# Logsumexp over heads: two more constant products on TensorE, the checks of three batches and one logarithm moved into or behind the hand list, and the last rows planned anew

## The chip, the cores and the metric

The kernel runs on one core of a Trainium2 chip. The metric is the device time of one execution in microseconds (us). Input and output lie in the chip's HBM; a core has TensorE (PE in the profile, its weight loads PEld), VectorE (DVE), ScalarE (ACT), GpSimd (POOL) and SyncE (SP, which here only issues transfers). Each engine works through its own instructions in order.

## The reference

`x` is 8 x 2048 x 2048 in f32 (134 MB), `bias` 8 x 256. A row of 2048 numbers is 8 heads of 256:

```python
B, S, D = x.shape
H = bias.shape[0]
Dh = D // H
x_heads = x.reshape(B, S, H, Dh).transpose(0, 2, 1, 3)
x_heads = x_heads + bias[None, :, None, :]
x_tiled = np.repeat(x_heads, 2, axis=2)
mx = x_tiled.max(axis=-1, keepdims=True)
lse = mx.squeeze(-1) + np.log(np.exp(x_tiled - mx).sum(axis=-1))
```

For each row and head: the logarithm of the sum of exp(x + bias) over 256 numbers, written twice. The output is 8 x 8 x 4096 in f32, 1 MB.

## The kernel before

**Units and loads.** The 16,384 rows are cut into 64 units of 256 rows (two rows on each of 128 partitions, 2 MB), eight units for a batch. They pass through four tiles `xb` of two units each. Units 2 to 41 (`BLOCKS` = 42) come as 4 MB loads of two units, so the last 4 MB block is units 40 and 41; units 42 to 56 come as 2 MB, 57 to 60 row by row as 1 MB, and 61 to 63 (`T_TAIL` = 61) in the parts of `TAIL_LOADS` (unit, row of the pair, first head, last head). All loads are issued on SP's queue, each once the unit that had its buffer is done.

**One unit of the bulk (units 0 to 53).** Nothing is subtracted ahead of the exponential. The eight heads go three ways:

- Heads 0 to 2: TensorE puts the bias into PSUM (`put_bias`, L356, a product of a matrix of ones with the bias, L370, issued a unit ahead) and adds x by a product with the identity (`late_heads`, L423, products L428). ACT takes the exponential from PSUM, head 0 with its sum (L439), heads 1 and 2 back into `xb` (L446).
- Heads 4 to 7: POOL adds the bias in place (`g_add`, L478).
- Head 3: no bias is added; ACT's exponential takes heads 3 to 7 in one instruction (L484), and DVE then multiplies head 3 by exp(bias), which lies in PSUM as `w_ps` (L496).

DVE sums heads 1 to 7 in one reduction (L503). So the order for a unit is: load; TensorE and POOL; ACT; DVE; its buffer is free.

**Later units.** 54 to 56 add fewer heads on TensorE; 57 to 60 go row by row: heads 0 and 1 as TensorE and ACT sums (L405, L459), the others as exponential (L484) and then multiplied by exp(bias) and summed by DVE (`weigh`, L519), with one head folded on POOL: multiplied (L536) and halved three times (L542), the last 32 numbers summed by DVE (`add_folded`, L549). In these units `keep_warm` (L418) issues a product of the identity with 384 constant columns of the bias into `tp`, which nothing reads.

**The hand list.** The six rows of units 61 to 63 are called e, f (61), a, b (62), c, d (63), and `TAIL` gives the order in which their steps are issued. A word such as `add a:12` means heads 1 and 2 of row a. `add`: TensorE adds x to a bias that was put into a PSUM bank ahead of it (`next_bias`, L799; the addition L821). `sum`: ACT's exponential from PSUM with its sum (L459). `copy`: ACT's exponential from PSUM into `xb` (L832). `exp`: ACT's exponential in place (L484). `weigh`: DVE's multiplication with exp(bias) and sum. `whole`: DVE's sum of 256 numbers (L845; no word of the old list uses it). `fold .0` to `.3`: POOL's multiplication and halvings, `folded`: DVE's sum of what is left. `sums`, `rest`: work left from unit 60. `warm`: `keep_warm`.

**Logarithms and stores.** The sums of batches 0 to 3 and 4 to 5 (the "groups") are turned by TensorE into `tp` and put through ACT's logarithm by `finish` (L564, the logarithm L578), two units after the group's last one; for batches 4 and 5 that is at unit 49. Batch 6 has its transposes in `turn_two` (L708) behind unit 57 and its logarithm in `finish_two` (L720) behind unit 58, in a bank of the PSUM tiles `pair`. Batch 7 is `finish_last` (L728), after the list: a transpose of the 128 x 128 sums, the logarithm, and a store on ACT's queue. `on_bank` enters the users of a bank, so that users of the other bank of the same tile don't wait for each other; the transpose in `finish_last` is not entered. `store` (L580) issues the stores of the groups and of `res_two` (batch 6) on SP's queue ahead of the list.

**Checks.** Without a maximum subtracted, a sum could overflow or vanish. So the exponent bits of all sums are looked at: `ends_of` (L592) reduces a group's bits to their largest and smallest on DVE and puts these two words beside the sums of the next group; `see_before` (`seen6`) looks at batch 6 with its two extra words, `see_early` (`seen7`) at the units of batch 7 that are done by then, `judge` (L642) at the rest; `gather` (L622) counts the odd bits by products with ones, and if there are any, `all_again` (L662) computes the whole output anew in the safe way. The verdict is loaded by SP and the others at the end.

Of the kernel before, what the change touches and what calls it, by code (L numbers as in the profile page):

```python
# [9 lines left out]
F32 = mybir.dt.float32  # L10
# [9 lines left out]
BLOCKS = 42  # L20
# [36 lines left out]
    (62, 1, 2, 8),  # L57
    (63, 1, 1, 6),
    (62, 0, 0, 5),
    (63, 1, 6, 8),  # L60
    (62, 0, 5, 8),
    (63, 0, 5, 8),
    (63, 1, 0, 1),
    (63, 0, 2, 5),
    (63, 0, 0, 2),
    (62, 1, 0, 1),
    (62, 1, 1, 2),
# [5 lines left out]
sums  add e:0  warm  exp e:1234567  # L73
rest  seen6  sums  fold e:67.0  weigh e:1  sum e:0
weigh e:2  add f:01  exp f:34567  weigh e:3  weigh e:4
fold e:67.1  weigh e:5  add f:2  sum f:0  seen7  weigh f:7  sum f:1
fold e:67.2  exp b:34567  weigh f:3  fold e:67.3  add b:2  weigh f:4
weigh f:5  weigh f:6  sum f:2  fold b:67.0  weigh b:3
add d:1  warm  exp d:2345  weigh b:4  weigh b:5
folded e:67  sum b:2  weigh d:2  fold b:67.1  sum d:1  weigh d:3  add a:12  # L80
exp a:34  weigh d:4  fold b:67.2  weigh d:5  exp d:67
weigh a:3  fold b:67.3  add a:0  seen  copy a:12  weigh a:4  weigh d:7
exp a:567  fold a:12.1  weigh d:6
folded b:67  sum a:0  weigh a:7  fold a:12.2  exp c:567  add d:0  weigh a:5
fold a:12.3  weigh a:6  sum d:0  weigh c:5  fold c:7.0  add c:2
exp c:34  weigh c:6  folded a:12  add c:0  exp c:1  fold c:7.1  weigh c:3
sum c:2  weigh c:4  fold c:7.2  add b:0  exp b:1  weigh c:1  fold c:7.3  sum c:0
weigh b:1  sum b:0  folded c:7
# [4 lines left out]
def kernel(  # L93
# [44 lines left out]
    odd = sb.tile([P, 2 + NR + H * SEEN], I32, name="odd")  # L138
# [8 lines left out]
    pads = [1] * (len(widths) - 1) + [0]  # L147
# [19 lines left out]
    sb.tile([P, 48], F32, name="gap")  # L167
# [412 lines left out]
    def store():  # L580

        for (b0, b1), r in zip(groups, res):
            nc.sync.dma_start(
                out=out[b0:b1].rearrange("b h (n r) -> (b h n) r", n=NB),
                in_=r.rearrange("q p k r -> q (p k r)"),
            )
        nc.sync.dma_start(
            out=out[B - 2].rearrange("h (n r) -> (h n) r", n=NBLK),
            in_=res_two.rearrange("q p k r -> q (p k r)"),
        )  # L590
# [44 lines left out]
    def see_before():  # L635
        odd_bits(odd[:, 0 : 2 + NR], Rx[len(groups)].bitcast(I32))

    def see_early():
        to = odd[:, 2 + NR :].rearrange("p (h c) -> p h c", h=H)
        odd_bits(to, last_bits(0, SEEN))  # L640
# [79 lines left out]
    def finish_two():  # L720
        (bank,) = two_in
        two = ps[bank][0 : H * NBLK]
        tv = bass.AP(
            tensor=two.tensor, offset=two.offset, ap=[two.ap[0], [1, P], [P, K], [0, 2]]
        )
        on_bank(bank, nc.scalar.activation(out=res_two, in_=tv, func=ACT.Ln))

# [131 lines left out]
    for t in range(T_TAIL):  # L859
# [4 lines left out]
        for k0, k1, c0, c1 in pieces(t):  # L864
# [4 lines left out]
            if m["late"]:  # L869
                pe_part = late_heads(m, t, bias_here, sums)  # L870
            else:
# [50 lines left out]
            if m["g0"] < H:  # L922
# [3 lines left out]
                if m["late"]:  # L926
                    bias_there = put_bias(*next_units.pop(0))
            else:
                for_pe.extend(pe_parts)

        for i, (_, b1) in enumerate(groups):
            if t - 2 == b1 * NBLK - 1:
                finish(i)
                ends_of(i)
        if t == T - 7:
            turn_two()
        if t == T - 6:
            finish_two()
# [9 lines left out]
    for what, row, heads, step in tail:  # L948
        if row is None:
# [3 lines left out]
                "seen6": see_before,  # L953
                "seen7": see_early,
                "seen": lambda: gather(odd, True, False),
# [5 lines left out]
    assert not for_pe and not for_pool and not to_bias  # L961
    finish_last()
# [35 lines left out]
```

## Time and profile before

| | |
|---|---|
| median of 3 runs | 322.71 us (322.35 to 322.72) |
| the profiled execution | 322.78 us |
| its span, first to last instruction | 321.0 us |
| its mean granted TensorE clock | 0.945 of full speed |
| busy: PE, DVE, ACT, POOL | 77%, 89%, 82%, 90% |
| read from HBM, written | 134.23 MB, 1.05 MB; 421 GB/s over the span |

Times are in us from the first instruction of the profiled execution. A row of the timeline is: start, length, engine, line, operation, output<-inputs, count, and in brackets the idle time before it with what ended it. A row of the chain of waits is: start, length, what. A row of busy time by stretch is: stretch, its length, the busy time of each engine with its instructions, the granted TensorE clock (1.00 is full speed), the share of time in which the DMA engines were busy, and GB/s. A row of a group of instructions is: what, count, then its busy time and the mean ns of one, then the idle time before them. The last loads wait in SP's queue for their buffers long before they move, so their time from issue to landing says little by itself; where a load lands is seen by the instruction that waits for it.

### The profile page before, as it was taken

How to read it: one execution, taken by the hardware profiler on the slowest of the kernel's cores; microseconds unless marked ns; L12 is line 12 of the kernel's file. 1: busy time of each engine (PE TensorE's matmuls, PEld its weight loads, DVE VectorE, ACT ScalarE, POOL GpSimd, SP SyncE). 2: the span in 40 equal slices, each digit the busy share in tenths (PEclk: the TensorE clock that was granted, in tenths of full speed). 3: DMA queues.
4: the chain of work that ended last, by engine and by line, in shares of the span. 5: the costliest groups of instructions: out<-in, count | busy, mean ns of one | idle time of the engine just before them, and what ended most of it. 6: DMA issues, size and time to landing. Idle time of an engine off the chain costs nothing.

```text
span 321.0 us, 2284 instructions
## 1 busy us (share of the span) xinstructions
PE 247.9 (77%) x618; PEld 100.3 (31%) x618; DVE 286.6 (89%) x304; ACT 264.0 (82%) x437; POOL 287.5 (90%) x116
## 2 busy tenths in 40 slices
PE   5998784867868687866979776698877788398773
PEld 2333331323323233322323332233332233143232
DVE  2347999699998989999799999979999999999996
ACT  1159986888879878888698988869988898999995
POOL 7939997999999999999999989999999999977874
PEclk9979998999979989997797999969999999979999
DMA  7999999999999999999999999999999999999995
GB/s 309 464 404 457 416 434 451 396 457 445 404 453 433 422 447 400 453 445 405 453 434 421 449 419 433 423 427 431 435 435 430 423 431 432 422 429 428 422 413 193
DMA packets 8950, 135.44 MB, mean 422 GB/s; under 512 B 996, under 2 KB 1511, under 8 KB 2791
## 3 DMA queue, kind: packets, MB, share of 16 engines
q1 hardware_dynamic: 8784, 135.14, 98.4%
q10 hardware_dynamic: 152, 0.14, 0.1%
q8 instruction: 5, 0.08, 0.1%
q14 instruction: 9, 0.07, 0.1%
HBM read 134.23 MB, written 1.05 MB: 421 GB/s over the span
## 4 chain that ended last, share of the span: by engine, by line
DVE 44%; DMA 34%; PE 11%; ACT 6%; POOL 3%; issue 1%; SPq 0%
DMA xb<-in_x_dram 34%; DVE R L503 30%; DVE xb L519 9%; DVE xb L496 4%; PE pair L428 4%; ACT xb L484 4%; PE one_ps L428 3%; POOL xb L478 3%; PE pair L303 1%; ACT xb L446 1%; PE pair L370 1%; PE one_ps L370 1%; DVE R L598 1%; DMA brow<-in_bias_dram 1%; DVE R L549 0%
## 5 line engine op out<-in xcount | busy, mean ns | idle before, releaser
L478 POOL TENSOR_TENSOR xb<-xb,b_rep 128x2048 f32<-128x2048 f32 x57 | 257.6, 4543 | 19.5 <-DMA xb<-in_x_dram 19.4
L503 DVE TENSOR_REDUCE R<-xb 128x14 f32<-128x3584 f32 (+1 forms) x57 | 216.8, 3804 | 1.9
L484 ACT ACTIVATE xb<-xb 128x2560 f32<-128x2560 f32 (+8 forms) x79 | 156.9, 1998 | 17.0 <-POOL xb L478 16.9
L428 PE MATMUL pair<-xb,ident 128*128 128x512 f32 x216 | 111.5, 642 | 0.0
L428 PE MATMUL one_ps<-xb,ident 128*128 128x512 f32 x108 | 63.0, 668 | 17.6 <-DMA xb<-in_x_dram 17.5
L446 ACT ACTIVATE xb<-pair 128x1024 f32<-128x1024 f32 x54 | 55.5, 1028 | 19.2 <-PE pair L428 19.1
L428 PEld LDWEIGHTS pair<-xb,ident 128*128 128x128 f32 x216 | 45.4, 210 | 59.2 <-issue 59.2
L496 DVE TENSOR_TENSOR xb<-xb,w_ps 128x512 f32<-128x512 f32 x54 | 36.7, 680 | 23.2 <-ACT xb L484 23.2
L370 PE MATMUL one_ps<-b,ones_bf 128*128 128x512 bf16 x52 | 20.1, 387 | 36.2 <-ACT xb L439 36.1
L439 ACT ACTIVATE xb<-one_ps 128x256 f32<-128x256 f32 x108 | 40.0, 379 | 7.0 <-PE one_ps L428 7.0
L370 PEld LDWEIGHTS <-ones_bf 128*128 128x128 bf16 (+1 forms) x174 | 17.5, 101 | 84.5 <-issue 77.6
L370 PE MATMUL pair<-b,ones_bf 128*128 128x512 bf16 x104 | 31.2, 381 | 0.0
L428 PEld LDWEIGHTS one_ps<-xb,ident 128*128 128x128 f32 x108 | 19.5, 198 | 32.7 <-DMA xb<-in_x_dram 26.5
L439 ACT ACTIVATION_READ_ACCUMULATOR xb<-one_ps 128x1 f32 x108 | 22.1, 205 | 0.0
L519 DVE CUSTOM_DVE_ANT_0 xb<-xb,w_ps 128x256 f32<-128x256 f32 x60 | 22.0, 414 | 0.0
L405 PE MATMUL pair<-xb,ident 128*128 128x512 f32 x28 | 16.0, 672 | 6.0 <-DMA xb<-in_x_dram 5.9
L542 POOL TENSOR_TENSOR xb<-xb 128x128 f32<-128x128 f32 (+3 forms) x36 | 14.2, 394 | 3.3 <-ACT xb L832 0.5
L459 ACT ACTIVATE xb<-pair 128x256 f32<-128x256 f32 x39 | 15.2, 417 | 0.0
L536 POOL TENSOR_TENSOR xb<-xb,w_sb 128x256 f32<-128x256 f32 (+1 forms) x11 | 9.1, 828 | 4.6 <-ACT xb L484 4.1
L821 PE MATMUL pair<-xb,ident 128*128 128x256 f32 (+1 forms) x22 | 8.0, 456 | 3.3 <-DMA xb<-in_x_dram 3.1
L459 ACT ACTIVATION_READ_ACCUMULATOR xb<-pair 128x1 f32 x39 | 9.6, 245 | 0.0
L405 PEld LDWEIGHTS pair<-xb,ident 128*128 128x128 f32 x28 | 4.9, 197 | 12.4 <-DMA xb<-in_x_dram 10.3
(61 smaller groups left out, 84.8 us busy)
## 6 DMA issues: line engine op xcount, KB each, us to landing
xb<-in_x_dram SPq DMA_DIRECT2D x20, 4096.0 KB, 22.3
xb<-in_x_dram SPq DMA_DIRECT2D x17, 2048.0 KB, 21.6
xb<-in_x_dram SPq DMA_DIRECT2D x10, 1024.0 KB, 21.1
xb<-in_x_dram SPq DMA_DIRECT2D x2, 640.0 KB, 18.1
xb<-in_x_dram SPq DMA_DIRECT2D x3, 384.0 KB, 12.3
xb<-in_x_dram SPq DMA_DIRECT2D x1, 768.0 KB
xb<-in_x_dram SPq DMA_DIRECT2D x2, 256.0 KB, 15.4
out_dram<-res SPq DMA_DIRECT2D x1, 512.0 KB, 5.8
```

The lines of the kernel that those rows point to most:

```text
L370: nc.tensor.matmul(p, lhsT=lhsT, rhs=each_row(b, h * Dh, Dh, K), start=i == 0, stop=False,)
L405: mm = nc.tensor.matmul(p, lhsT=ident, rhs=xts[t % NBUF][:, ka:kb, c : c + w], start=False, stop=True,)
L428: mm = nc.tensor.matmul(p, lhsT=ident, rhs=xts[t % NBUF][:, :, h * Dh : (h + 1) * Dh], start=False, stop=True,)
L439: act = nc.scalar.activation(out=xts[t % NBUF][:, k, 0:Dh], in_=got[0][:, k * Dh : (k + 1) * Dh], func=ACT.Exp, accum_out=sums[:, k, 0:1],)
L446: act = nc.scalar.activation(out=xts[t % NBUF][:, :, Dh : m["pe"] * Dh].rearrange("p k (h j) -> p h k j", j=Dh), in_=got[-1].rearrange("p ...
L459: act = nc.scalar.activation(out=xts[t % NBUF][:, k, h * Dh : (h + 1) * Dh], in_=p, func=ACT.Exp, accum_out=sums[:, k, h : h + 1],)
L478: add = nc.gpsimd.tensor_tensor(out=v, in0=v, in1=each_row(b_rep, c - G0, D - c, k1 - k0), op=ALU.add)
L484: return on_x(t, nc.scalar.activation(out=v, in_=v, func=ACT.Exp), [after])
L496: mul = nc.vector.tensor_tensor(out=f, in0=f, in1=each_row(w_ps, m["pe"] * Dh - W0, n, k1 - k0), op=ALU.mult,)
L503: red = nc.vector.tensor_reduce(out=sums[:, k0:k1, h0:H], in_=v.rearrange("p k (h j) -> p k h j", j=Dh), op=ALU.add, axis=mybir.AxisListTy ...
L519: ttr = nc.vector.tensor_tensor_reduce(out=v, in0=v, in1=w, scale=1.0, scalar=0.0, op0=ALU.mult, op1=ALU.add, accum_out=dst,)
L542: done = nc.gpsimd.tensor_tensor(out=v[:, :, 0:n], in0=v[:, :, 0:n], in1=v[:, :, n : 2 * n], op=ALU.add)
```

## The change

Four things are done.

1. At unit 39, the last one ahead of the last 4 MB block, `keep_warm` is issued twice: once behind that unit's identity products (`late_heads`) and once behind the bias products for unit 40 (`put_bias`).
2. The checks of batches 4 and 5 no longer go through two end words. `ends_of` is called for the first group alone (after unit 33), so its pair of reductions behind unit 49 goes. In the list, `seen5` (`see_groups`) turns the 258 words of batches 4 and 5 (their sums and the two end words of batches 0 to 3) in place into their odd bits; by then their logarithm is long taken. `seen6` (`see_two`) takes the 128 words of batch 6; `seen` (`gather_seen`) gathers both. `odd` and the sums of batch 6 are two words shorter each, and the unused tile `gap` grows from 48 to 64 words, so that `xb` lies at the address that it had.
3. `turn_two` and `finish_two` are called after the list, just ahead of `finish_last`, and the store of batch 6 with them: it is no longer issued by `store` ahead of the list.
4. `TAIL_LOADS` and `TAIL` are new. In numbers of instructions: 30 `weigh` become 29 and 2 `whole`, with 4 `folded` in both; 11 `sum`, 11 `exp` and 1 `copy` become 9, 12 and 3; 15 steps of `fold` become 14; 11 `add` (13 heads) become 12 (15 heads); the 2 `warm` go. The parts of `TAIL_LOADS` remain 13, with the same 6 MB; the first two (rows e and f) stay.

```diff
--- before.py
+++ after.py
@@ -54,38 +54,39 @@
 TAIL_LOADS = [
     (61, 0, 0, 8),
     (61, 1, 0, 8),
-    (62, 1, 2, 8),
-    (63, 1, 1, 6),
-    (62, 0, 0, 5),
-    (63, 1, 6, 8),
-    (62, 0, 5, 8),
-    (63, 0, 5, 8),
-    (63, 1, 0, 1),
-    (63, 0, 2, 5),
+    (63, 1, 2, 8),
+    (62, 0, 2, 8),
+    (62, 1, 2, 6),
+    (63, 0, 4, 8),
+    (63, 1, 0, 2),
+    (62, 1, 6, 8),
+    (62, 1, 1, 2),
+    (62, 0, 0, 2),
+    (63, 0, 2, 4),
+    (62, 1, 0, 1),
     (63, 0, 0, 2),
-    (62, 1, 0, 1),
-    (62, 1, 1, 2),
 ]
 
 ROWS = {"e": (61, 0), "f": (61, 1), "a": (62, 0), "b": (62, 1), "c": (63, 0), "d": (63, 1)}
 
 TAIL = """
-sums  add e:0  warm  exp e:1234567
-rest  seen6  sums  fold e:67.0  weigh e:1  sum e:0
-weigh e:2  add f:01  exp f:34567  weigh e:3  weigh e:4
-fold e:67.1  weigh e:5  add f:2  sum f:0  seen7  weigh f:7  sum f:1
-fold e:67.2  exp b:34567  weigh f:3  fold e:67.3  add b:2  weigh f:4
-weigh f:5  weigh f:6  sum f:2  fold b:67.0  weigh b:3
-add d:1  warm  exp d:2345  weigh b:4  weigh b:5
-folded e:67  sum b:2  weigh d:2  fold b:67.1  sum d:1  weigh d:3  add a:12
-exp a:34  weigh d:4  fold b:67.2  weigh d:5  exp d:67
-weigh a:3  fold b:67.3  add a:0  seen  copy a:12  weigh a:4  weigh d:7
-exp a:567  fold a:12.1  weigh d:6
-folded b:67  sum a:0  weigh a:7  fold a:12.2  exp c:567  add d:0  weigh a:5
-fold a:12.3  weigh a:6  sum d:0  weigh c:5  fold c:7.0  add c:2
-exp c:34  weigh c:6  folded a:12  add c:0  exp c:1  fold c:7.1  weigh c:3
-sum c:2  weigh c:4  fold c:7.2  add b:0  exp b:1  weigh c:1  fold c:7.3  sum c:0
-weigh b:1  sum b:0  folded c:7
+sums  add e:01  exp e:34567
+seen5  add e:2  rest  copy e:01  seen6  weigh e:7
+sums  weigh e:3  fold e:01.1  sum e:2  weigh e:4  add f:01
+exp f:34567  weigh e:5  fold e:01.2  weigh e:6
+seen7  fold e:01.3  add f:2  copy f:01  folded e:01  fold f:67.0  weigh f:3
+weigh f:4  exp d:34567  weigh f:5  add d:2
+whole f:0  fold f:67.1  whole f:1  sum f:2  weigh d:7
+sum d:2  weigh d:3  fold f:67.2  add a:2  exp a:34567  weigh d:4
+fold f:67.3  weigh d:5  weigh d:6  sum a:2
+add b:2  seen  folded f:67  fold a:67.0  weigh a:3  exp b:345  weigh a:4
+weigh a:5  sum b:2  weigh b:3  exp c:56  fold a:67.1
+weigh b:4  weigh b:5  add d:01  exp c:7  weigh c:5  exp c:4
+fold a:67.2  exp b:67  weigh c:7  fold a:67.3  weigh c:6
+copy d:01  add b:1  weigh b:7  exp a:1  add a:0  fold d:01.1  weigh c:4
+sum b:1  weigh b:6  exp c:23  weigh a:1  add b:0  fold d:01.2
+sum a:0  folded a:67  weigh c:2  fold d:01.3  add c:0  exp c:1  weigh c:3  sum b:0
+weigh c:1  sum c:0  folded d:01
 """
 
 
@@ -135,7 +136,7 @@
     NR = KB * H * NB
     SEEN = (T_TAIL - (B - 1) * NBLK) * K
     LATE = NBLK * K - SEEN
-    odd = sb.tile([P, 2 + NR + H * SEEN], I32, name="odd")
+    odd = sb.tile([P, NR + H * SEEN], I32, name="odd")
     odd_last = sb.tile([P, H * LATE], I32, name="odd_last")
     verdict = sb.tile([1, 1], F32, name="verdict")
 
@@ -144,7 +145,7 @@
         starts.append(min(starts[-1] + P // (H * NB), B - 2))
     groups = list(zip(starts, starts[1:]))
     widths = [(b1 - b0) * NR for b0, b1 in groups] + [NR, NR]
-    pads = [1] * (len(widths) - 1) + [0]
+    pads = [1] * len(groups) + [0, 0]
     Rx = [
         sb.tile([P, pad + n + pad], F32, name=f"R{i}")
         for i, (n, pad) in enumerate(zip(widths, pads))
@@ -164,7 +165,7 @@
     ]
     res_two = sb.tile([H * NBLK, P, K, 2], F32, name="res_two")
     res_last = sb.tile([P, P, 2], F32, name="res_last")
-    sb.tile([P, 48], F32, name="gap")
+    sb.tile([P, 64], F32, name="gap")
     xbs = [sb.tile([P, KB, D], F32, name=f"xb{i}") for i in range(NBUF // TB)]
     xts = [xb[:, k : k + K] for xb in xbs for k in range(0, KB, K)]
     w_ps = pp.tile([P, W2 - W0], F32, name="w_ps")
@@ -584,10 +585,6 @@
                 out=out[b0:b1].rearrange("b h (n r) -> (b h n) r", n=NB),
                 in_=r.rearrange("q p k r -> q (p k r)"),
             )
-        nc.sync.dma_start(
-            out=out[B - 2].rearrange("h (n r) -> (h n) r", n=NBLK),
-            in_=res_two.rearrange("q p k r -> q (p k r)"),
-        )
 
     def ends_of(i):
 
@@ -632,11 +629,21 @@
                 stop=stop,
             )
 
-    def see_before():
-        odd_bits(odd[:, 0 : 2 + NR], Rx[len(groups)].bitcast(I32))
+    def see_groups():
+
+
+        v = Rx[len(groups) - 1].bitcast(I32)
+        odd_bits(v, v)
+
+    def see_two():
+        odd_bits(odd[:, 0:NR], sums_in[len(groups)].bitcast(I32))
+
+    def gather_seen():
+        gather(Rx[len(groups) - 1].bitcast(I32), True, False)
+        gather(odd, False, False)
 
     def see_early():
-        to = odd[:, 2 + NR :].rearrange("p (h c) -> p h c", h=H)
+        to = odd[:, NR:].rearrange("p (h c) -> p h c", h=H)
         odd_bits(to, last_bits(0, SEEN))
 
     def judge():
@@ -724,6 +731,10 @@
             tensor=two.tensor, offset=two.offset, ap=[two.ap[0], [1, P], [P, K], [0, 2]]
         )
         on_bank(bank, nc.scalar.activation(out=res_two, in_=tv, func=ACT.Ln))
+        nc.sync.dma_start(
+            out=out[B - 2].rearrange("h (n r) -> (h n) r", n=NBLK),
+            in_=res_two.rearrange("q p k r -> q (p k r)"),
+        )
 
     def finish_last():
         bank = n_ps[0] % len(ps)
@@ -868,6 +879,8 @@
             bias_here = bias_there
             if m["late"]:
                 pe_part = late_heads(m, t, bias_here, sums)
+                if t == BLOCKS - TB - 1:
+                    keep_warm()
             else:
                 heads = add_x(m, t, k0, c0, c1, bias_here)
 
@@ -925,17 +938,16 @@
                     first_factors()
                 if m["late"]:
                     bias_there = put_bias(*next_units.pop(0))
+                    if t == BLOCKS - TB - 1:
+                        keep_warm()
             else:
                 for_pe.extend(pe_parts)
 
         for i, (_, b1) in enumerate(groups):
             if t - 2 == b1 * NBLK - 1:
                 finish(i)
-                ends_of(i)
-        if t == T - 7:
-            turn_two()
-        if t == T - 6:
-            finish_two()
+                if i + 1 < len(groups):
+                    ends_of(i)
     store()
     last_bank = heads[0][2]
     to_read[last_bank] = len(for_pe)
@@ -950,15 +962,18 @@
             {
                 "sums": sum_before,
                 "rest": lambda: flush(for_pool),
-                "seen6": see_before,
+                "seen5": see_groups,
+                "seen6": see_two,
                 "seen7": see_early,
-                "seen": lambda: gather(odd, True, False),
+                "seen": gather_seen,
                 "warm": keep_warm,
             }[what]()
         else:
             tail_step(what, *row, heads, step)
         next_bias()
     assert not for_pe and not for_pool and not to_bias
+    turn_two()
+    finish_two()
     finish_last()
     again = judge() > 0
 
```

## The prediction, made before the changed kernel ran

> **What bounds the kernel now.** I read the head of the page first, then the busy time by stage, then the chain of waits, then the timeline around the two places the chain points to.
>
> ```profile
> span 321.0 us, 2284 instructions
> ```
> ```profile
> core 0: us, PE busy (x) PEld busy (x) DVE busy (x) ACT busy (x) POOL busy (x), PEclk, DMA share, GB/s
> 180.00:217.00 37.00, 28.53 (x67) 11.19 (x66) 34.39 (x18) 30.52 (x46) 34.88 (x8) 0.91 1.00 429
> 217.00:260.00 43.00, 33.51 (x94) 14.34 (x93) 42.66 (x22) 39.45 (x61) 43.00 (x11) 1.00 1.01 430
> 300.00:315.00 15.00, 11.28 (x43) 5.36 (x42) 15.00 (x89) 15.00 (x40) 11.66 (x22) 1.00 1.02 414
> ```
>
> The DMA engines are full in every stage (share 1.00 to 1.02), so transfers pace the bulk: DVE still has 2.6 us to spare in 180 to 217. From 217 on DVE has none (42.66 of 43, 15.00 of 15), and in the last 15 us ACT has none either. The chain says what made DVE late at 217:
>
> ```profile
> 208.02 2.07 PE one_ps L428 x2
> 210.09 3.43 PE pair L428 x4
> 213.52 0.02 issue
> 213.54 1.02 ACT xb L446
> 214.57 2.24 ACT xb L484
> 216.81 0.02 issue
> 216.83 0.70 DVE xb L496
> 217.53 0.02 issue
> 217.55 3.89 DVE R L503
> ...
> 257.56 0.65 DVE R L598 x2
> ```
>
> Unit 40 (the last 4 MB load holds units 40 and 41) lands at 208.02, and TensorE needs 5.5 us for its bias products. From 216.83 the chain is DVE alone, to its last reduction at 317.31 below. So today DVE sets the end; the data are a close second.
>
> **The products ahead of the last 4 MB block.** PE busy time and granted clock by stretches of 3.41 us, the steps in which the recorded clock changes:
>
> ```profile
> 166.15:169.56 3.41, 1.70 (x6) 0.49 (x4) 3.38 (x3) 3.11 (x8) 2.80 (x2) 1.00 0.91 394
> 169.56:172.97 3.41, 3.41 (x5) 1.33 (x4) 3.38 (x3) 3.09 (x6) 3.41 (x1) 0.50 1.02 442
> 193.45:196.87 3.42, 1.77 (x6) 0.67 (x5) 3.42 (x2) 3.42 (x6) 3.42 (x1) 1.00 1.04 450
> 196.87:200.28 3.41, 2.41 (x8) 0.96 (x6) 3.38 (x2) 2.89 (x3) 2.92 (x2) 1.00 1.05 452
> 203.69:207.11 3.42, 1.55 (x5) 0.29 (x3) 3.38 (x3) 3.27 (x6) 3.42 (x1) 1.00 0.86 369
> 207.11:210.52 3.41, 2.50 (x3) 1.17 (x4) 3.41 (x2) 2.73 (x4) 2.80 (x2) 0.50 1.01 432
> ```
>
> The first number behind the length is PE's busy time, the third from the end the clock. A stretch with 1.55 or 1.70 us of PE work is followed by half clock, one with 1.77 by full clock, so the limit is near 1.7. The change adds a constant product in each of the two idle gaps before unit 40:
>
> ```profile
> 206.09 0.38 PE L370 MATMUL one_ps<-b,ones_bf 128*128 128x512 bf16 x1 [1.66 <-ACT xb L439]
> 206.31 0.59 PE L370 MATMUL pair<-b,ones_bf 128*128 128x512 bf16 x2
> 208.02 1.22 PE L428 MATMUL one_ps<-xb,ident 128*128 128x512 f32 x1 [1.12 <-DMA xb<-in_x_dram]
> ```
> ```profile
> 188.84 1.12 PE L428 MATMUL one_ps<-xb,ident 128*128 128x512 f32 x2 [1.15 <-DMA xb<-in_x_dram]
> 188.87 9.03 POOL L478 TENSOR_TENSOR xb<-xb,b_rep 128x2048 f32<-128x2048 f32 x2 [1.03 <-DMA xb<-in_x_dram]
> ```
> ```profile
> L419 PE MATMUL tp<-b_rep,ident 128*128 128x384 f32 x20 | 8.1, 485 | 0.0
> ```
>
> The 20 records of L419 are 10 products of two passes, 8.1 us in all: 0.81 each. The gaps are 1.66 and 1.12, so they cost nothing: idle TensorE covers them (without that cover, 0.81 in front of unit 40). The stretch before 207.11 rises from 1.55 to about 2.5 us (0.81 plus the start of the second), well above 1.7. At full clock two products take 1.12 (188.84) where unit 40's took 2.07, so its 5.5 us become 3.0, done by about 211.0 instead of 213.5. The next one to be late is POOL: two additions in 9.03 are 4.51 each, and they start 0.03 behind TensorE, so unit 40's ends at 212.56; ACT's exponential (2.24 above, 2.32 below) then lets DVE start at about 214.95 instead of 216.83. Gain in DVE's lead: 1.9, bounded by 0 (clock falls all the same) and 1.9 (POOL).
>
> In sentences of their own: the Trainium skill, page "TensorE: Matmul & The Clock Gate", Part 1, says that the clock is judged over free-running windows of 3413 ns; the clock column steps by that length, so the trace agrees, and where the windows fall may differ from run to run. The same page's section "Why this matters for your kernels" asks only that there be no idle gap over about 3 us; here gaps of 1.66 and 1.12 sufficed, so the row decides. By that rule the products would change nothing; that is rival B.
>
> **The removed end reductions, and a new wait.** The pair at L598 goes: 0.65 off DVE. But the lead does not carry past batch 5's logarithm:
>
> ```profile
> 253.10 0.41 PE L568 MATMUL tp<-ident,R 128*64 128x128 f32 x2 [0.31 <-DVE R L503]
> ```
> ```profile
> 253.55 1.02 ACT L578 ACTIVATE res<-tp 64x1024 f32<-64x1024 f32 x1 [0.92 <-PE tp L568]
> 254.47 2.32 ACT L484 ACTIVATE xb<-xb 128x2560 f32<-128x2560 f32 x1
> ```
>
> DVE's multiplication behind the pair (at 257.56 + 0.65 = 258.21) needs the exponential that ends at 256.8, and this is held by ACT's logarithm, which waits for PE's transposes. With DVE early only the 0.31 of PE's wait goes, so this exponential ends at 256.5 at the earliest. DVE, ready at 258.21 less 1.9 less 0.65 = 255.7, waits some 0.9 there. The lead after it is 1.4 with the exponential as before, 1.7 with all of the 0.31 gone; I take 1.45, as ACT's work ahead of the logarithm stays.
>
> **DVE's work in the list.** The old list has 30 weighings and 4 folded sums, the new one 29, 2 whole reductions and 4 folded sums.
>
> ```profile
> 305.79 0.85 DVE L608 TENSOR_SCALAR odd<-R 128x130 int32<-128x130 int32 x1
> 306.56 0.41 DVE L519 CUSTOM_DVE_ANT_0 xb<-xb,one_ps 128x256 f32<-128x256 f32 x1
> 306.90 0.08 DVE L519 DVE_READ_ACCUMULATOR2_ANT R<- 128x1 f32 x1
> ```
>
> One weighing is 0.34 from its start to the next (306.56 to 306.90). A whole reduction of 256 has no row; it lies between 0.28 (256 of the 3584 words that take 3.89 in the chain) and the 0.41 of a weighing; with 0.34 the list is 0.34 longer. The check of batch 6 cost 0.77 (305.79 to 306.56) for 130 words. The new checks do 258 and 128 words: 0.45 together if the time goes with the words at the reduction's 1.09 ns and the rest was an overhead met once, 1.1 if the second costs what the old one did, so -0.3 to +0.35. DVE's last reduction: 317.31 - 1.45 + 0.34 - 0.3 to + 0.35, that is 315.9 to 316.55.
>
> **The data, and the new end.** In 300 to 315 the queue moves 414 GB/s at share 1.02, and the tail loads the same 6 MB in another order.
>
> ```profile
> L726 ACT ACTIVATE res_two<-pair 64x512 f32<-64x512 f32 x1 | 0.6, 607 | 0.0
> ```
> ```profile
> 314.90 0.30 PEld L821 LDWEIGHTS pair<-xb,ident 128*128 128x128 f32 x2 [0.25 <-DMA xb<-in_x_dram]
> 314.90 0.70 PE L821 MATMUL pair<-xb,ident 128*128 128x256 f32 x2
> ...
> 316.35 0.47 ACT L459 ACTIVATE xb<-pair 128x256 f32<-128x256 f32 x1
> ...
> 317.31 0.17 DVE L549 TENSOR_REDUCE R<-xb 128x1 f32<-128x32 f32 x1
> ...
> 317.63 0.30 PE L731 MATMUL pair<-ident,R 128*128 128x128 f32 x1 [1.49 <-DVE R L549]
> ...
> 317.97 0.38 ACT L737 ACTIVATE res_last<-pair 128x256 f32<-128x256 f32 x1 [1.05 <-PE pair L731]
> ```
>
> The addition at 314.90 waited for row c's last 256 KB; two loads of 128 KB followed, 0.32 us each at 414 GB/s: the last lands at 315.5. In the new order the last is c's heads 0 and 1, at 315.5 too. From there: addition of head 0 0.05 + 0.70 (316.25), its sum on ACT 0.47 (316.72), then the logarithm of batch 6, 0.61, which now stands here (317.33). Its two transposes (0.30 each at most, by L731's) run while ACT sums. The last transpose isn't entered as a user of its bank, so the built program has it wait for that logarithm: 0.30 and 0.04 to the last logarithm, which starts at about 317.7. DVE's branch, 316.55 + 0.66 as now (317.31 to 317.97), reaches 317.2 at most and no longer decides. Against 317.97 that is -0.27.
>
> The store of batch 6 moves from the middle of SP's queue to its end, just ahead of the store on ACT's queue. Behind it SP has only the verdict's load. If the two stores of 128 KB share the engines, 0 to 0.32; I take 0.05. ACT has the same 48 heads in 24 instructions instead of 23, with two sums fewer, and POOL one fold step fewer: nothing for either, as both lists end in a wait for data.
>
> Sum: -0.27 + 0.05 = -0.2 on a profiled execution of 322.78 (span 321.0 and 1.8 around it), which stands 0.07 above the median of 322.71 of the runs. That gives about **322.5**; own range 322.1 to 322.9.
>
> **Rivals.** *A, slower: TensorE's clock falls in the tail.* The list loses both its constant products. Between about 307 and 310.4 the new order has only the additions of d's and a's head 2 (0.70 each) and the bias products around them, some 1.8 us of PE work by these rows, at the limit of 1.7; the old list has, in the stretches 306.09 to 309.51 and after, the products in it. If a clock window lies there, the last additions run at half clock, 2.07 for 1.12 as at 208.02, a factor of 1.85: 0.6 more for the last addition, 0.3 for the two transposes, 0.25 for the last one, +1.2, so 323.7 (0.7 if the window ends earlier). Against it: with the windows where this profile has them, 306.09 and 309.51, the two additions and f's tail add up to over 2 us. Chance 0.28.
>
> *B, the products don't lift the clock.* Then DVE keeps only the 0.65: last reduction at 317.31 - 0.65 + 0.34 - 0.3 to + 0.35 = 316.7 to 317.35, last logarithm 317.4 to 318.0, time 322.5 to 322.85, centre 322.7. Chance 0.12.
>
> *C, the data come earlier.* Now DVE hides any earlier landing; in the new kernel it would count. 0.5 us earlier (0.5% of the last 100 us of transfers), and DVE's branch at 316.6 to 317.2 bounds it: -0.75, so 322.0. For it: the queue's share fell to 0.86 in the stretch from 203.69, so it is not full at every moment, and buffers that DVE frees earlier could fill such holes. Against it: each stage as a whole stands at 1.00 to 1.02. Chance 0.25.
>
> **How the numbers follow.** The forecast has 0.35. What this kernel's measurement can tell from no change is 0.2%, 0.65 us: below 322.06 is faster, above 323.36 slower. Forecast and B lie within these but for 0.05 below and 0.02 above; of A all 0.28 is slower, of C 0.22 faster: faster 0.27, same 0.43, slower 0.30. The range reaches into C and through most of A: 321.9 to 323.9.
>
> **What would show it.** Right: clock 1.0 at 208 to 214, unit 40's DVE start near 215.0, a DVE wait of about 0.9 near 256 behind the logarithm of batch 5, DVE idle before its last operations, the last transpose released by ACT's logarithm of batch 6 and the last logarithm near 317.7. Wrong: half clock in 310 to 316 (A) or at 208 (B), a last landing far from 315.5 (C), or DVE again without a gap to the end.

## The result, and the profile after

The changed kernel takes 323.43 us (median of 9 executions, 323.12 to 323.89) against 322.59 (9 executions, 322.28 to 322.90) for the kernel before: a ratio of 1.0029, 95% interval 1.0020 to 1.0038. It is 0.84 us slower. The forecast was 322.5, 0.2 us faster. The time lies above the forecast's own range (322.1 to 322.9) and inside the wider one that takes in the rivals (321.9 to 323.9), on the other side of no change.

The profiled execution took 323.16 us, 0.38 more than that of before. Its page, and its busy time by the same stretches as in the prediction, with the tail (length, then PE, PEld, DVE, ACT and POOL busy, the granted clock, the DMA share, GB/s):

```profile
span 321.3 us, 2297 instructions
```
```profile
203.69:207.11 3.42, 2.44 (x9) 1.03 (x7) 3.13 (x3) 3.07 (x6) 3.42 (x1) 1.00 0.85 364
207.11:210.52 3.41, 2.93 (x8) 1.17 (x8) 3.38 (x3) 3.06 (x5) 2.81 (x2) 1.00 1.04 447
210.52:213.93 3.41, 3.37 (x10) 1.42 (x9) 3.41 (x1) 2.53 (x2) 3.41 (x2) 1.00 1.01 432
...
306.09:309.51 3.42, 2.34 (x10) 1.17 (x9) 3.42 (x17) 3.38 (x8) 3.00 (x5) 1.00 1.00 415
309.51:312.92 3.41, 2.37 (x19) 1.16 (x19) 3.41 (x20) 3.41 (x9) 2.48 (x5) 1.00 1.04 400
312.92:316.33 3.41, 3.24 (x16) 1.77 (x14) 3.41 (x19) 3.41 (x13) 2.46 (x5) 1.00 0.94 362
```

The products did what they were said to do: the stretch ahead of 207.11 has 2.44 us of TensorE work instead of 1.55, and the clock is 1.00 through unit 40, where it was 0.50. It is 1.00 in the tail too, up to 318.5, when the last transpose is done. So in this profile neither of the two rivals on the clock is seen. The timeline of DVE, from unit 40 to its last reduction:

```profile
214.80 0.69 DVE L497 TENSOR_TENSOR xb<-xb,w_ps 128x512 f32<-128x512 f32 x1 [0.52 <-ACT xb L485]
...
256.14 0.69 DVE L497 TENSOR_TENSOR xb<-xb,w_ps 128x512 f32<-128x512 f32 x1 [0.62 <-ACT xb L485]
...
288.11 2.29 DVE L504 TENSOR_REDUCE R<-xb 128x8 f32<-128x2048 f32 x1 [0.83 <-ACT xb L485]
...
304.62 0.29 DVE L605 TENSOR_SCALAR R<-R 128x258 int32<-128x258 int32 x1
304.83 0.17 DVE L550 TENSOR_REDUCE R<-xb 128x1 f32<-128x32 f32 x1
304.92 0.21 DVE L605 TENSOR_SCALAR odd<-R 128x128 int32<-128x128 int32 x1
305.06 0.94 DVE L520 CUSTOM_DVE_ANT_0 xb<-xb,w_sb 128x256 f32<-128x256 f32 x1
305.93 0.08 DVE L520 DVE_READ_ACCUMULATOR2_ANT R<- 128x1 f32 x1
...
307.30 0.94 DVE L605 TENSOR_SCALAR odd<-R 128x80 int32<-128x80 int32 x1
308.16 0.21 DVE L550 TENSOR_REDUCE R<-xb 128x2 f32<-128x64 f32 x1
...
314.88 0.60 DVE L520 CUSTOM_DVE_ANT_0 xb<-xb,w_sb 128x256 f32<-128x256 f32 x1
315.40 0.08 DVE L520 DVE_READ_ACCUMULATOR2_ANT R<- 128x1 f32 x1
...
317.58 0.21 DVE L550 TENSOR_REDUCE R<-xb 128x2 f32<-128x64 f32 x1
```

The same steps in the kernel before (its start of unit 40, 216.83, stands in the prediction):

```profile
258.13 0.68 DVE L496 TENSOR_TENSOR xb<-xb,w_ps 128x512 f32<-128x512 f32 x1
...
289.19 2.28 DVE L503 TENSOR_REDUCE R<-xb 128x8 f32<-128x2048 f32 x1
...
305.69 0.18 DVE L549 TENSOR_REDUCE R<-xb 128x1 f32<-128x32 f32 x1
```

DVE reaches unit 40 at 214.80 instead of 216.83, and after its wait at 256 it stands at 256.14 where it stood at 258.13: 1.99 us ahead. Two things take that away. First, a wait for ACT at 288.11; before, the same reduction started at 289.19, so 1.08 is left. Second, the list. From the end of the last weighing of unit 60 to the last reduction DVE needs 12.96 us (304.62 to 317.58), where it needed 11.62 (305.69 to 317.31), without a gap between its rows in either. The sum closes: 317.31 - 1.08 + 1.34 = 317.57.

Three long rows make up more than the 1.34. A weighing of 256 numbers, 0.34 to the next elsewhere, takes 0.87 at 305.06 and 0.52 at 314.88; a check of 80 words takes 0.86 at 307.30, where it took 0.11 before. That is 1.46 too much; the rest of the list is 0.1 shorter. What POOL did at those moments (start, length):

```profile
304.99 0.73 POOL L543 TENSOR_TENSOR xb<-xb 128x256 f32<-128x256 f32 x1 [0.75 <-ACT xb L843]
...
306.90 1.28 POOL L537 TENSOR_TENSOR xb<-xb,w_sb 128x512 f32<-128x512 f32 x1 [0.19 <-ACT xb L485]
...
314.20 0.99 POOL L543 TENSOR_TENSOR xb<-xb 128x256 f32<-128x256 f32 x1 [0.57 <-ACT xb L843]
```

Each long DVE row starts while such a fold step runs and ends shortly behind it. The steps end at 305.72, 308.18 and 315.19; the next DVE instruction starts at 305.93, 308.16 and 315.40. Taking off what each instruction needs by itself (0.34, 0.11, 0.34) DVE was let in at 305.59, 308.05 and 315.06, each time 0.13 before the end of POOL's row. All three read nothing from PSUM: both inputs of the weighings of head 7 are in SBUF (`w_sb`), and the check goes from SBUF to SBUF. The weighings of the other heads read their factor from PSUM (`w_ps`, `one_ps`), and run beside POOL at 0.34. DVE's plain reductions have one input and go from SBUF to SBUF as well, and they do not wait: the two of 256 numbers, here beside three halvings on POOL, take 0.65 together, and 0.65 or 0.66 in every profile of the new order below, wherever POOL's steps stand.

```profile
309.31 0.73 DVE L856 TENSOR_REDUCE R<-xb 128x1 f32<-128x256 f32 x2
```
```profile
308.26 1.65 POOL L543 TENSOR_TENSOR xb<-xb 128x256 f32<-128x256 f32 x3
```

In the kernel before, the row of 0.85 that the prediction showed stood in the same way behind POOL:

```profile
305.28 1.27 POOL L536 TENSOR_TENSOR xb<-xb,w_sb 128x512 f32<-128x512 f32 x1 [0.68 <-ACT xb L484]
```

It ends at 306.55, and DVE's next instruction started at 306.56. The end, on TensorE:

```profile
315.60 0.69 PE L832 MATMUL pair<-xb,ident 128*128 128x256 f32 x2
316.13 0.38 PE L720 MATMUL pair<-ident,R 128*64 128x128 f32 x2
317.94 0.30 PE L742 MATMUL pair<-ident,R 128*128 128x128 f32 x1 [1.43 <-DVE R L550]
```

The last addition, at 315.60, is where the prediction had it (315.5 and 0.05), but the last transpose waits for DVE, to 317.94.

### The profile page after: what moved, and what is told of

Read it like the earlier page. It is cut to its first block, busy times and chain, and to the rows that moved or that the text cites. A ratio compares the mean times of both kernels' runs of the same rounds, so it can differ in the third digit from the quotient of the medians.

```text
span 321.3 us, 2297 instructions
## 1 busy us (share of the span) xinstructions
PE 244.8 (76%) x626; PEld 99.4 (31%) x627; DVE 287.7 (90%) x303; ACT 264.8 (82%) x436; POOL 287.3 (89%) x115
## 4 chain that ended last, share of the span: by engine, by line
DMA 42%; DVE 21%; POOL 18%; ACT 9%; PE 8%; issue 0%; SPq 0%
DMA xb<-in_x_dram 42%; POOL xb L479 18%; DVE R L504 10%; DVE xb L520 7%; ACT xb L485 7%; PE pair L429 2%; PE one_ps L429 2%; DVE xb L497 2%; PE pair L304 1%; PE pair L371 1%; ACT xb L447 1%; PE one_ps L371 1%; DMA brow<-in_bias_dram 1%; ACT xb L440 1%; ACT xb L460 0%; DVE R L550 0%
## 5 line engine op out<-in xcount | busy, mean ns | idle before, releaser
L485 ACT ACTIVATE xb<-xb 128x2560 f32<-128x2560 f32 (+7 forms) x80 | 155.9, 1960 | 20.6 <-POOL xb L479 20.6
L429 PE MATMUL pair<-xb,ident 128*128 128x512 f32 x216 | 107.3, 621 | 0.0
L429 PEld LDWEIGHTS pair<-xb,ident 128*128 128x128 f32 x216 | 44.2, 205 | 58.0 <-issue 58.0
L406 PE MATMUL pair<-xb,ident 128*128 128x512 f32 x28 | 16.3, 685 | 7.6 <-DMA xb<-in_x_dram 7.4
L460 ACT ACTIVATE xb<-pair 128x256 f32<-128x256 f32 x37 | 14.1, 403 | 0.0
L537 POOL TENSOR_TENSOR xb<-xb,w_sb 128x256 f32<-128x256 f32 (+1 forms) x10 | 8.4, 840 | 3.7 <-ACT xb L485 3.2
L832 PE MATMUL pair<-xb,ident 128*128 128x256 f32 (+1 forms) x24 | 9.1, 472 | 3.3 <-DMA xb<-in_x_dram 3.2
L406 PEld LDWEIGHTS pair<-xb,ident 128*128 128x128 f32 x28 | 5.0, 204 | 15.2 <-DMA xb<-in_x_dram 13.2
L460 ACT ACTIVATION_READ_ACCUMULATOR xb<-pair 128x1 f32 x37 | 8.5, 229 | 0.0
```

The costliest lines, as they stand in the source:

```text
L406: mm = nc.tensor.matmul(p, lhsT=ident, rhs=xts[t % NBUF][:, ka:kb, c : c + w], start=False, stop=True,)
L429: mm = nc.tensor.matmul(p, lhsT=ident, rhs=xts[t % NBUF][:, :, h * Dh : (h + 1) * Dh], start=False, stop=True,)
L460: act = nc.scalar.activation(out=xts[t % NBUF][:, k, h * Dh : (h + 1) * Dh], in_=p, func=ACT.Exp, accum_out=sums[:, k, h : h + 1],)
L485: return on_x(t, nc.scalar.activation(out=v, in_=v, func=ACT.Exp), [after])
```

## The experiments

Eleven runs, each with the times of the kernel before on the same chip beside it:

| run | median us | before us | ratio (95% interval) |
|---|---|---|---|
| e1, factor of head 7 in PSUM | 322.61 | 322.44 | 1.0006 (0.9997 to 1.0015) |
| e2, the change again | 323.61 | 322.44 | 1.0035 (1.0022 to 1.0049) |
| e3, the change, clear of POOL | 322.66 | 322.44 | 1.0011 (1.0002 to 1.0020) |
| e4, before, checks moved | 322.35 | 322.44 | 1.0001 (0.9992 to 1.0010) |
| e5, e3 with the logarithm early | 322.52 | 322.27 | 1.0002 (0.9993 to 1.0011) |
| e6, before with the products | 322.19 | 322.27 | 0.9994 (0.9985 to 1.0003) |
| e7, the change without the products | 323.13 | 322.27 | 1.0025 (1.0016 to 1.0035) |
| e8, the change with the old lists | 322.85 | 322.27 | 1.0012 (1.0003 to 1.0021) |
| e9, before, products and checks moved | 322.27 | 322.32 | 0.9995 (0.9986 to 1.0004) |
| e10, before, logarithm late | 322.92 | 322.32 | 1.0017 (1.0008 to 1.0026) |
| e11, e10 without the store of batch 6 | 322.19 | 322.27 | 0.9996 (0.9987 to 1.0005) |

**e1: where the factor lies.** Theory: a weighing with both inputs in SBUF, or a check from SBUF to SBUF, waits for POOL's running step. Rival: the long rows are late data or a late ACT.

```diff
             w = w_sb[:, c - W1 : c - W1 + Dh]
+            if t >= T_TAIL:
+                w = w_ps[:, W1 - W0 : W2 - W0]
```

> The changed kernel, but the weighings of head 7 in the last six rows read their factor from PSUM (that of head 6, so these heads' sums are wrong) instead of from SBUF. Theory, SBUF sharing: a DVE instruction that reads both inputs from SBUF, or moves SBUF to SBUF as the checks do, waits for the running POOL instruction. Then the weighing of head 7 in row e falls from 0.94 to 0.41 and that of row c from 0.60 to 0.41, while the check of early batch 7 (0.94) may still stall; DVE ends some 0.5 to 0.7 earlier than 317.8 and the time falls by as much, to 322.8 to 323.0. Rival, late data or ACT: the long rows stay where they are, and so does the time, 323.4.

322.61: 0.8 below the change (1.0 below its repeat on the same chip, e2), more than was expected, and level with before. In its trace each weighing of head 7 takes 0.33 to 0.35 to the next, also beside a running fold step, though the order and the data are those of the change. The checks, still from SBUF to SBUF, wait: that of early batch 7, as was foreseen, and that of batch 6, which did not wait in the change's profile. The second, in DVE's timeline:

```profile
305.28 0.75 DVE L607 TENSOR_SCALAR odd<-R 128x128 int32<-128x128 int32 x1
305.95 0.41 DVE L522 CUSTOM_DVE_ANT_0 xb<-xb,w_ps 128x256 f32<-128x256 f32 x1
```

The order of the steps is the same and only the place of an operand differs, so the theory holds for the weighings. But this profile is of the slowest of the run's 11 executions (323.12): its last reduction starts at 317.59, no earlier than in the change, and the checks wait 1.1 in it. Where the typical execution gains its 0.8 no trace shows.

**e2: the change again**, with no edit.

> The changed kernel unaltered, beside the others on the same chip. Theory: the same three long DVE rows (0.94, 0.94, 0.60) stand where POOL runs a fold step, the median is again 0.6 to 1.0 above before, and single executions again differ by about 0.7. If the profile falls on a slower execution, its clock row shows where TensorE ran at half speed; if the long rows are an accident of one execution, they are gone here.

323.61 (323.17 to 323.98). The profile shows an execution of 323.87, and in DVE's timeline the long rows have moved:

```profile
305.47 0.76 DVE L605 TENSOR_SCALAR odd<-R 128x128 int32<-128x128 int32 x1
...
307.86 0.78 DVE L605 TENSOR_SCALAR odd<-R 128x80 int32<-128x80 int32 x1
...
314.58 0.85 DVE L520 CUSTOM_DVE_ANT_0 xb<-xb,w_sb 128x256 f32<-128x256 f32 x1
```

Now the check of batch 6 waits (0.21 in the first profile), and e's weighing of head 7 behind it takes 0.41. DVE came to the list 0.55 later (305.17 for 304.62), after a wait of 1.23 at 288.66, and so met POOL elsewhere: which instructions collide depends on some tenths of a microsecond. The number of waits, three, stayed; that they would stand at the same rows was wrong.

The collisions are not what makes this execution slower than the first profile's, though. The list took 13.06 here and 12.96 there. The 0.55 comes for the most part from TensorE's clock, which was half from 277.5 to 284.3 here and from 281.6 to 285.1 there: here ACT waited for TensorE's additions, and its exponential, and with it DVE's reduction, came late.

```profile
284.62 0.38 ACT L460 ACTIVATE xb<-pair 128x256 f32<-128x256 f32 x1 [0.36 <-PE pair L406]
```

At the end the clock was half again from about 318.5 on, and the last transpose took 0.45 for 0.30. Together 0.55, 0.10 and 0.15 are the 0.80 by which the last logarithm is later (319.07 for 318.27).

**e3: the change, clear of POOL.** Only DVE's words move in the list.

```diff
-seen5  add e:2  rest  copy e:01  seen6  weigh e:7
+add e:2  weigh e:7  rest  copy e:01
...
-seen7  fold e:01.3  add f:2  copy f:01  folded e:01  fold f:67.0  weigh f:3
+fold e:01.3  add f:2  copy f:01  seen5  folded e:01  fold f:67.0  weigh f:3
...
-whole f:0  fold f:67.1  whole f:1  sum f:2  weigh d:7
+whole f:0  fold f:67.1  whole f:1  sum f:2
...
-fold f:67.3  weigh d:5  weigh d:6  sum a:2
+fold f:67.3  weigh d:5  weigh d:6  seen6  seen7  weigh d:7  sum a:2
```

> The changed kernel with five DVE words of the list at other places, where POOL was idle in the trace: the weighing of e's head 7 first, the check of batches 4 and 5 behind POOL's third halving of row e, the checks of batches 6 and 7 and the weighing of d's head 7 near 310. Theory, SBUF sharing: the rows of 0.94 fall to 0.2 to 0.45, DVE ends its list 1.0 to 1.4 earlier or waits for data, the last logarithm starts at 317.6 to 317.8 and the time falls to 322.3 to 322.7. Rival, late data or ACT set these rows: the waits appear in other rows and the time stays at 323.2 to 323.5.

322.66, again 0.8 below the change (0.95 below e2), and within the expected 322.3 to 322.7. The three waits are gone. DVE's last reduction starts at 316.37, 1.2 earlier. Now the end is as the prediction had worked it out, on TensorE:

```profile
317.33 0.33 PE L742 MATMUL pair<-ident,R 128*128 128x128 f32 x1 [0.82 <-ACT res_two L733]
```

The transpose waits for the logarithm of batch 6, and the last logarithm starts at 317.70. So taking DVE's waits out of the list gives 0.8 to 1.0 back, and then ACT and its logarithm set the end. e1 gives as much, though in its one trace the checks still wait. Without the waits the change is level with before or 0.1% slower, still not faster.

**e4: before, with its checks moved** behind `weigh f:4`, to where POOL was idle.

> The kernel before with the check of batch 6 and of early batch 7 a few DVE instructions later, to where POOL was idle. Theory, SBUF sharing: the check of 0.85 falls to about 0.2, DVE ends 0.5 to 0.7 earlier, and the data (last landing 315.5) then set the end: 0.2 to 0.5 faster than before, 322.1 to 322.4. Rival, the 0.85 is this instruction's own cost for 130 words: nothing changes, 322.6.

The long row is gone (both checks together take 0.25), and DVE's last reduction starts at 316.83 instead of 317.31. Not all of that is the check's doing: DVE also came to the list 0.85 earlier than in the profile of before, and then had short gaps in it. The time is that of before (322.35 against 322.44); the 0.2 to 0.5 that were expected did not come. ACT now ends last; TensorE's last transpose:

```profile
317.17 0.33 PE L731 MATMUL pair<-ident,R 128*128 128x128 f32 x1 [0.88 <-ACT xb L459]
```

The prediction's "DVE sets the end; the data are a close second" left out that ACT is as close.

**e5: e3 with the logarithm of batch 6 at its old place.**

```diff
+        if t == T - 7:
+            turn_two()
+        if t == T - 6:
+            finish_two()
...
-    turn_two()
-    finish_two()
     finish_last()
```

> The changed kernel with the DVE words clear of POOL as in the third experiment, and the transposes, the logarithm and the store of batch 6 at the places that they had before the change. Theory: with DVE out of the way the end is held by ACT's logarithm of batch 6, which the last transpose waits for; without it there the transpose follows the last sum (end near 316.7), the last logarithm starts at 317.1 to 317.3 instead of 317.70, and the time is 0.4 to 0.6 below the third experiment: 322.0 to 322.3. Rival: ACT, full from 289 on, pays the 0.6 back earlier in the list, and the time stays at 322.6.

322.52, not faster than e3 by more than can be told, so the time is the rival's. Its cause is not shown. The last sum on ACT starts at 316.72 instead of 316.32, but ACT also came later to its exponentials ahead of the list (285.32 instead of 284.89), behind a wait of 0.34 for TensorE as in e2. And what the last transpose waits for is DVE, whose last reduction starts at 317.07:

```profile
317.43 0.30 PE L742 MATMUL pair<-ident,R 128*128 128x128 f32 x1 [1.18 <-DVE R L550]
```

**e6: before with the two products and nothing else** (the two calls of `keep_warm` at unit 39).

> The kernel before with nothing but the two constant products ahead of the last 4 MB block. Theory: unit 40 runs at full clock, DVE gains 1.5 to 2.0 us ahead of the list and ends at 316.0 to 316.8, ACT's last sum and the data then hold the last logarithm near 317.5, and the time is 322.1 to 322.4, 0.1 to 0.4 below before. Rival, the products do not lift the clock: as before, 322.4 to 322.6. If the earlier DVE meets other POOL steps, the gain is less than that, and the long rows say so.

322.19 against 322.27: no difference that can be told. The clock stays full through unit 40 (its half-speed stretch lies earlier, from 198.4 to 201.8); but DVE's gain ends at 288, as in the change:

```profile
288.16 2.29 DVE L503 TENSOR_REDUCE R<-xb 128x8 f32<-128x2048 f32 x1 [0.70 <-ACT xb L484]
```

and at the end the chain of waits is ACT alone from 307.78 on:

```profile
316.16 0.73 ACT xb L459 x4
316.89 0.04 issue
316.93 0.34 PE pair L731
317.27 0.02 issue
317.30 0.38 ACT res_last L737
```

**e7: the change without the products.**

> The changed kernel without the two constant products. Theory: DVE has a lead of only 0.65 (the removed reductions) and the list's longer work and waits remain: last DVE reduction at 318.0 to 318.4, time 323.4 to 323.9, no faster than the change and perhaps 0.3 slower. Rival, the products are what costs (in front of unit 40, or by a shifted phase): then this one is faster than the change, 322.5 to 322.8.

323.13, 0.3 below the first theory's place and 0.3 above the rival's. Its ratio, 1.0025, cannot be told from those of the change (1.0029 and, in e2, 1.0035), so the products neither cost nor gain anything that can be told. The clock is half for one stretch of 3.4 us, from 207.6, where it was half for two in the profile of before, and DVE starts unit 40 at 215.63, 0.8 later than in the change. Yet it waits for ACT to 288.31, nearly where it waits with the products, and then has three long rows (0.77, 0.78, 0.60). So the lead that the products give is not kept to the list.

**e8: the change with the old lists**, its two checks both at the place of the old one.

> The changed kernel with the old orders of loads and steps of the last rows; the checks of batches 4 and 5 and of batch 6 stand where the old check of batch 6 stood. Theory, the new order put DVE's SBUF-only instructions where POOL runs: here only one check meets a fold step, DVE ends by 316.8, the logarithm of batch 6 behind ACT's last sum holds the last logarithm at 317.7 to 317.9, time 322.4 to 322.7. Rival, the slowness comes from the products, the checks or the moved logarithm: time 323.2 to 323.6 as with the change.

322.85, between the two theories' places, a little over the first. The weighings of head 7 run at 0.41 or 0.42 as in the old kernel, but one check meets a fold step of 512 as it begins:

```profile
305.26 1.30 DVE L604 TENSOR_SCALAR odd<-R 128x128 int32<-128x128 int32 x1
```

DVE's last reduction starts at 317.24, where 316.8 at the latest was expected, and the last transpose waits for it. The new lists are then worth some 0.0017 of the ratio (1.0012 against 1.0029). They are not the whole loss, but in this profile the rest too holds a wait for POOL, of 1.1.

**e9: e4 and e6 together.**

> The kernel before with the two constant products and with the checks of batch 6 and early batch 7 where POOL was idle: the two edits that each took DVE off the end, together. Theory: DVE no longer decides in either, ACT's last sum and the data do, so the two do not add: last logarithm at 317.2 to 317.5, time 322.0 to 322.3, 0.0 to 0.3 below before. If DVE's lateness were still the limit, they would add to 0.5 or more: below 321.9.

322.27: they do not add, as expected. ACT sets the end here too (the profile is of the slowest execution, 322.85). No version here beats the kernel before by more than can be told.

**e10: before with the logarithm and the store of batch 6 behind the list.**

```diff
-        if t == T - 7:
-            turn_two()
-        if t == T - 6:
-            finish_two()
...
+    turn_two()
+    finish_two()
     finish_last()
```

> The kernel before with nothing but the transposes, logarithm and store of batch 6 moved behind the list. Theory: ACT's logarithm of 0.6 behind its last sum (end 316.8) and the last transpose behind it put the last logarithm at 317.8 to 318.0 at the earliest, about where DVE holds it in the slower executions of before and 0.3 to 0.4 later than in the faster ones: time 322.4 to 322.8, 0.1 to 0.4 above before. Rival: ACT is 0.6 earlier through the whole list, and the move costs nothing: 322.2 to 322.4.

322.92, 0.6 above before, more than expected, and not in the way that was expected. The last logarithm starts at 317.37, as in e6 (317.30), since here its transpose falls into the other tile of `pair` and waits for ACT's last sum only. Yet the span is 0.7 longer than that of e6. The DMA issues say where it is (queue, KB, us from issue to landing):

```profile
out_dram<-res_two SPq DMA_DIRECT2D x1, 128.0 KB, 2.5
out_dram<-res_last ACTq DMA_DIRECT2D x1, 128.0 KB, 2.4
```

The store of batch 7 took 2.4 instead of the 1.8 that it takes in the kernel before. It was issued at 317.79, and that of batch 6 at 317.34.

**e11: e10 without the store of batch 6.**

> The tenth experiment (the transposes and the logarithm of batch 6 behind the list, nothing else changed) without the store of batch 6, so that batch 6 is missing in the output. Theory, the two stores share the way out: the store of batch 7 lands 1.8 after its issue again instead of 2.4, and the time falls by about 0.6 to 322.2 to 322.4. Rival, ACT's logarithm at the end is what costs: the time stays at 322.8 to 323.0.

322.19: all of it is back, with the logarithm still behind the list.

```profile
out_dram<-res_last ACTq DMA_DIRECT2D x1, 128.0 KB, 1.8
```

So what costs in e10 is the second store close ahead of the last one. In the change and in e2 the two are issued 1.4 and more apart and the last one lands in 1.7, in e3 0.8 apart and in 1.8: there this store costs nothing, because the list or the logarithm has made the last store late.

## Why the prediction was wrong

**The products** (lead 1.9, no cost): right against the one execution that the prediction looked at. Unit 40 ran at full clock, as in all eight profiles with the products, DVE started it at 214.80 where 214.95 was forecast, and e6 shows no cost. But the half clock at unit 40 is not what the kernel without them always has. Of five profiles without the products, two have it (before and e7); in e4, e10 and e11 the clock is 1.00 from 207 to 214. In e10 TensorE has nearly the gaps that the prediction showed, and DVE starts unit 40 when it does in the change:

```profile
205.86 0.38 PE L370 MATMUL one_ps<-b,ones_bf 128*128 128x512 bf16 x1 [1.50 <-ACT xb L439]
...
207.83 1.13 PE L428 MATMUL one_ps<-xb,ident 128*128 128x512 f32 x2 [1.16 <-DMA xb<-in_x_dram]
...
214.80 0.69 DVE L496 TENSOR_TENSOR xb<-xb,w_ps 128x512 f32<-128x512 f32 x1 [0.29 <-ACT xb L484]
```

So the 1.9 is there to be won in some executions only. The limit near 1.7, read from three stretches, does not hold either: in the same profile of before the stretch from 271.96 to 275.37 has 1.66 us of TensorE work, and the next one runs at full clock.

**The wait at 256**: right in place and cause (0.62 for 0.9), and the lead behind it was 1.99, not 1.45. But the prediction took it as the last wait before the list. There was a second one, at 288, which it did not look for. POOL's additions show why it must be there, before and after:

```profile
276.08 4.54 POOL L478 TENSOR_TENSOR xb<-xb,b_rep 128x2048 f32<-128x2048 f32 x1 [0.30 <-DMA xb<-in_x_dram]
```
```profile
276.01 4.54 POOL L479 TENSOR_TENSOR xb<-xb,b_rep 128x2048 f32<-128x2048 f32 x1 [0.30 <-DMA xb<-in_x_dram]
```

The data for it land at the same time in both profiles, POOL and ACT follow at the same times, and DVE can be 1.1 ahead of the profile of before there and no more. In e2 and e5, where ACT waited for TensorE as well, it was 0.5 to 0.6 ahead. DVE waits for ACT at this place in every profile here but the one of before.

**DVE's work in the list**: this step failed, and it decided the outcome. The list was to be 0.04 to 0.69 longer. The prediction read the row of 0.85 for 130 words as "an overhead met once" and priced the checks by it at -0.3 to +0.35 around +0.34 for the reductions. The row was no price but a wait for POOL (in e4 both checks together take 0.25), and the question should have been which instructions of the new order can meet such a step. Measured, the list is 1.34 longer: the new checks of batches 4 to 6 are cheap (0.21 and 0.14 for 0.77: -0.42), two reductions for one weighing are +0.31, and three waits add 0.53, 0.75 and 0.18. e3 takes all three away, and 0.8 goes; e1 takes away those of the weighings by the place of an operand alone, and as much goes. The Trainium skill, page "SBUF — State Buffer", section "Who interferes with whom", states it: a DVE instruction with two inputs in SBUF, or a tensor_scalar in a mode that uses both port pairs, shares a port with GpSimd, and the one that starts second waits in full. The rows of the weighings agree, with the 0.13 above (in which mode the checks ran no row shows), and also the other way round: the fold step at 314.20 took 0.99 for 0.73, behind a weighing of head 7 that DVE had begun at 314.19.

**"DVE's branch ... no longer decides"** fell with it: 317.58 instead of 316.55 at most.

**The data and the new end**: right, and seen where DVE is out of the way (e3): last landing near 315.6, last logarithm at 317.70 behind that of batch 6.

**The store of batch 6**: bounds of 0 to 0.32 were too narrow; 0.7 was measured in e10. In the change it cost nothing, as the stores lie far apart.

**The starting point**: the sum was made against one execution of 322.78. The kernel before has since shown medians of 322.27 to 322.59, so that execution was one of its later ones. It is also the only profile here in which DVE is so late that it does not wait at 288. In a quicker execution ACT may be what ends last (as in e4), and then a lead for DVE is worth nothing; no quicker one of the kernel before itself was profiled. The 0.27 that the new end was to bring was counted from there, and e3, which has just this end, is not faster than before.

**The rivals.** A had the sign and the size, but not the cause: in the change's profile the clock stayed at 1.00 until TensorE was done, and in the tail of e2 only the last transpose ran at half clock, for 0.15. B and C did not come about. The slower case that did, DVE behind POOL, was not among them.

What stays open: why e5 is not faster than before, how the 0.8 is shared between the checks and the weighings in an average execution, and how often the kernel before meets half clock at unit 40.

## What to carry to other kernels

A row that is far too long for its size is a question, not a price: look at what the other engines did between its start and its end before taking its length into a sum. In an order written out by hand, DVE's products with both inputs in SBUF and checks like these have to be placed by POOL's steps as well as by their data, or, for the products, be given an operand in PSUM. When an engine gains a lead, follow it past every later wait for data; here 2.0 us gained at 214 were 1.1 at 288 and nothing at the end, since ACT ends there too. And a loss seen in one profiled execution may not be there in the next: the half clock at unit 40 was missing from three of five profiles without the products.

## What the runs showed of the hardware that was not expected

A DVE product with both inputs in SBUF, and a check (TENSOR_SCALAR) from SBUF to SBUF, waited for a running fold step of POOL and got on 0.13 us before the end of POOL's row in all three cases of the change; the wait is inside DVE's row, with no idle time beside it. The longest such row was 1.30 us for a check of 128 words that takes 0.21 when it is free. Reductions of one input from SBUF to SBUF did not wait (0.65 or 0.66 for two). Two stores of 128 KB from two queues, issued 0.45 us apart, held the second back to 2.4 us instead of 1.8; 0.8 apart it landed in 1.8.
